# Layer 0's MLP: up tiles in pairs by seven half-width products, with weight sums, token sums and another order of the work

## The chip, the cores and the metric

The kernel runs on one core of one Trainium2 chip. The metric is the device time of one execution in microseconds. Engines are named as in the profile: PE is TensorE, DVE VectorE, ACT ScalarE, POOL GpSimd, SP SyncE, whose queue issues the loads.

## The reference, cut to what matters

Two layers act on 512 latent tokens; the first also on 256 context tokens with the same weights. Each layer is a set of token mixers and then an MLP with a gated residual. D_MODEL is 1024, D_FF 4096, all in float32.

```python
def sq_relu_mlp(h, w1, b1, w2, b2):
    a = jax.nn.relu(h @ w1 + b1)
    return (a * a) @ w2 + b2
...
        h2 = rmsnorm(x, ln2_g[l]) * (1.0 + sc2) + sh2
        x = x + g2 * sq_relu_mlp(h2, mlp_w1[l], mlp_b1[l], mlp_w2[l], mlp_b2[l])
        if with_ctx_out:
            ...
            xc = xc + cg2 * sq_relu_mlp(hc2, mlp_w1[l], mlp_b1[l], mlp_w2[l], mlp_b2[l])
```

sc2, sh2 and g2 come from a modulation product `silu(c) @ w_mod`, done per layer.

## The kernel before, in words

Activations lie with features on the partitions and tokens along the row: 768 tokens in layer 0 (pieces of 512 and 256 columns, `segs`), 512 in layer 1. Each float32 operand is split in two parts of the type that PE takes at full pace: a high part `H` and the rest, `L`. A product is three matmuls per block of 128 features: H·bH, H·bL, L·bH. `low` (L187) makes the split: a cast to H on ACT (L193) and a subtraction to L (`tt`, L177) on DVE, or on POOL for weights.

`load` (L307) takes one of four raw buffers (pool `raw`), issues a DMA of 512 x 128 weights on SP (L315) and splits it into one of six pairs `wH`, `wL`. A raw buffer is free again when its split on POOL is done. `proj` (L323) runs the matmuls of one output tile: per weight load and per piece 12 matmuls of 512 or 256 columns (`mm`, L215).

`mlp` (L1740) runs over eight chunks c. `up(c)` makes four tiles f of 128 hidden features: two loads and 48 matmuls (`proj`); ReLU with bias out of PSUM on ACT (`mr`), the square on POOL (`mq`), and its `low` with H on ACT and L on DVE (`aL`). Then `down(c-1)` uses the four tiles of the chunk before: for each of eight output tiles m one load of 512 x 128 of w2, 24 matmuls, and `residual` (L180, two pieces) on DVE, which adds the gated result into `xs[m]`. The last chunk's down product (`down_last`) runs within the first strand of the next layer. PSUM tiles come from small rings: the two pieces of a tile take a buffer of `p2`, of which there are two, so the products of tile m wait until the residual of tile m-2 has read its buffer.

The order on each engine is the order in which generators (strands) yield: `pipe` (L1484) turns among up to nine strands, here the output projection, the norms and the MLP; `run` (L1570) puts in one filling unit (`fill_step`) after every so many steps. The units of `mods` are the products for the next layer's modulation: `mod_units` (L1923) makes for each block j loads of 512 x 128 of w_mod, products of 32 rows (`mod__m`, L217), and an ending step. `prefetch` issues loads of coming units ahead, into the same raw buffers.

Of the kernel before, what the change touches and what calls it, by code (L numbers as in the profile page):

```python
# [22 lines left out]
P = 128  # L23
# [82 lines left out]
def hybrid_block(ctx: ExitStack, tc: tile.TileContext, I, C, out, dbg=None, stop=None):  # L106
# [12 lines left out]
    def uid(s):  # L119
        cnt[0] += 1  # L120
        return f"{ph[0]}__{s}_{cnt[0]}"

    def slot(dt=F32, name="s"):
        return sp.tile([P, TOT], dt, tag="t", name=uid(name), bufs=NT)

    def big(dt=F32, name="s"):
        return sp.tile([P, 1024], dt, tag="s", name=uid(name), bufs=NS)
# [13 lines left out]
    def yslot():  # L141
        return sp.tile([P, TOT], F32R, tag="y", name=uid("y"), bufs=8)
# [7 lines left out]
    def acc_tile(segs, filler=False):  # L150

        if filler:
            return [(t0, n, pf1()[:, :n]) for t0, n in segs]
        w, t = span(segs), p2()
        return [(w.start, w.stop - w.start, t[:, w])]
# [20 lines left out]
    def tt(o, a, b, op, eng=None):  # L176
        (eng or nc.vector).tensor_tensor(o, a, b, op)  # L177
# [10 lines left out]
    def low(H, L, src, heng=None, leng=None):  # L188

        if heng is nc.vector:  # L190
            nc.vector.tensor_copy(H, src)
        else:
            nc.scalar.copy(H, src)  # L193
        tt(L, src, H.bitcast(F32), ALU.subtract, eng=leng)
# [13 lines left out]
    def mm(ps, a, b, start, stop_, pos=None):  # L208
        n = int(np.prod(ps.shape[1:]))
        if a.dtype == F32R:  # L210
            cost = n * (0.43e-3 if n >= 256 else 1.7e-3)
        else:
            cost = max(n * 1.7e-3, 0.214)
        if pos is None:
            in_order(nc.tensor.matmul(ps, lhsT=a, rhs=b, start=start, stop=stop_), cost)  # L215
        else:
            in_order(nc.tensor.matmul(ps, lhsT=a, rhs=b, start=start, stop=stop_, tile_position=pos),  # L217
                     cost * ps.shape[0] / P)
# [82 lines left out]
    def rawtile():  # L301
        return rp.tile([P, 512], F32, tag="raw", name=uid("raw"))
# [6 lines left out]
    def load(src):  # L309

        raw = rawtile().rearrange("p (k n) -> p k n", k=4)
        if callable(src):
            src(raw)
        else:
            newest[0] = nc.sync.dma_start(raw, src.rearrange("(k p) n -> p k n", p=P))  # L315
        H, L = whalf()
        low(H, L, raw, leng=nc.gpsimd)
        return H, L
# [1 line left out]
    def wcols(src, x):  # L320
        return src[512 * x : 512 * x + 512]

    def proj(pieces, halves, mov):  # L323

        last_ = len(halves) - 1
        for x, half in enumerate(halves):
            if half is None:
                continue
            H, L = half
            for t0, n, ap in pieces:  # L330
                for a, c in [(t0, n)] if n <= 512 else [(t0, 512), (t0 + 512, n - 512)]:
                    ps, q = ap[:, a - t0 : a - t0 + c], slice(a, a + c)
                    for k in range(4):
                        bH, bL = mov(4 * x + k)
                        mm(ps, H[:, k, :], bH[:, q], x == 0 and k == 0, False)
                        mm(ps, H[:, k, :], bL[:, q], False, False)
                    for k in range(4):
                        mm(ps, L[:, k, :], mov(4 * x + k)[0][:, q], False, x == last_ and k == 3)
                    yield 0.0

    def now(g):
# [134 lines left out]
    def norm_piece(xs, a, piece, made, done, sc, sh, hH, hL):  # L476

        while piece not in made:
            yield 0.3
        pbf = yield from rms_stat(xs, a, *piece)  # L480
        yield from norm_mod(xs, [piece], pbf, sc, sh, hH, hL)
        done.add(piece)
# [225 lines left out]
    def hview(hH, hL):  # L708
        return lambda k: (hH[:, k, :], hL[:, k, :])
# [1027 lines left out]
                residual(xs[k], part, modT[l][:, 16:24, :], k)  # L1737
            made.add((t0, n))

    def mlp(l, vt, xs, mov, segs, near_end, first2, pieces, made, tail):  # L1740

        w = span(segs)
        g2 = modT[l][:, 40:48, :]

        gb = const(f"g2b{l}", [P, 16])
        gbv = gb.rearrange("p (k v) -> p k v", v=2)
        tt(gbv, g2, vt[:, vbase["mlp_b2"] : vbase["mlp_b2"] + KD].unsqueeze(2).to_broadcast([P, KD, 2]), ALU.mult)
        def weights1(f):
            return [load(wcols(I["mlp_w1"][l][:, f * P : (f + 1) * P], h)) for h in range(2)]

        def up(c):
            a, early = [], []
            for j in range(4):
                f = c * 4 + j
                if c == 0 and j < 3:
                    if j == 0:
                        W3 = [weights1(i) for i in range(3)]
                        early = [acc_tile(segs) for i in range(2)]

                        def third():  # L1760

                            while cur[0] is not None or cur[2] is not None:
                                yield 0.2
                            held[0] = True
                            early.append(acc_tile(segs, True))
                            return early[2], W3[2]

                        yield from first2(early[:2], W3[:2], mov, third)
                    elif j == 2:
                        held[0] = False  # L1770
                    ps = early[j]
                else:
                    ps = acc_tile(segs)
                    W = weights1(f)
                    yield from proj(ps, W, mov)
                r, q = slot(name="mr"), slot(name="mq")
                evac(r, ps, lambda d, a: act(d, a, AF.Relu, bias=vcol(vt, "mlp_b1", f)))
                tt(q[:, w], r[:, w], r[:, w], ALU.mult, eng=nc.gpsimd)
                H, L = yslot(), big(F32R, "aL")
                low(H[:, w], L[:, w], q[:, w])  # L1780
                a.append((H, L))
            return a

        def weights2(c, m):
            return load(I["mlp_w2"][l][c * 512 : (c + 1) * 512, m * P : (m + 1) * P])

        def down(c, a):
            for m in range(KD):
                ps = acc_tile(segs)
                W = weights2(c, m)  # L1790
                yield from proj(ps, [W], lambda k: a[k])
                if c == 0:
                    for t0, n in segs:
                        v = 0 if t0 == 0 else 1
                        q = slice(t0, t0 + n)
                        ts(xs[m][:, q], xs[m][:, q], gbv[:, m, v : v + 1], None, ALU.add)
                residual(xs[m], ps, g2, m)

        def down_last(a):
            last2 = []  # L1800
            for m in range(KD):
                if m in (1, 6):
                    near_end(m == 6)
                W, ps = weights2(7, m), acc_tile(segs)
                if m < KD - 2:
                    yield from proj(ps, [W], lambda k: a[k])
                    residual(xs[m], ps, g2, m)
                else:
                    last2.append((m, W, ps))
            for t0, n in pieces:  # L1810
                for m, W, ps in last2:
                    part = [(t0, n, cutout(ps, t0, n))]
                    yield from proj(part, [W], lambda k: a[k])
                    residual(xs[m], part, g2, m)
                made.add((t0, n))

        prev = None
        for c in range(8):
            a = yield from up(c)
            if prev is not None:  # L1820
                yield from down(c - 1, prev)
            prev = a
        tail.append(down_last(prev))


# [94 lines left out]
        for k in range(KD):  # L1920
            after(nc.sync.dma_start(xd[k][:, w], xs[k][:, w]), newest[0])

    def mod_units(l, js):  # L1923
        blocks = [mod_block(l, vts[l], j) for j in js]
        us = list(blocks[0][0])
        for a, b in zip(blocks, blocks[1:] + [None]):
            if b is not None:
                us += b[0]
            us.append(a[1])
        return us  # L1930

    def norms(pieces, made, sc, sh, hH, hL):
        hdone.clear()
        a = slot(name="ssq")
        return [norm_piece(xs, a, p, made, hdone, sc, sh, hH, hL) for p in pieces]

    def then(done, pieces, f):
        while not all(p in done for p in pieces):
# [5 lines left out]
    for l in range(DEPTH):  # L1944
# [71 lines left out]
        ts(modT[l][:, 16:24, :], modT[l][:, 16:24, :], 0.5, None, ALU.mult)  # L2016
        ph[0] = f"out{l}"
        if l + 1 < DEPTH:
            mods.extend(mod_units(l + 1, range(4)))
        hH = hp.tile([P, KD, TOT], F32R, tag="hH", name=uid("hH"))  # L2020
        hL = hp.tile([P, KD, TOT], F32R, tag="hL", name=uid("hL"))
        pieces = segs if len(segs) > 1 else [(0, 256), (256, 256)]
# [8 lines left out]
                prefetch()  # L2031
            ph[0] = mine

        body = mlp(l, vt, xs, hview(hH, hL), segs, next_layer, by_pieces(pieces, hdone), pieces, made, tail)
        run(f"mlp{l}", pipe(before + [body], 9), pace=PACE["mlp"])
        drain()


# [62 lines left out]
```

## Time and profile before

| | |
|---|---|
| median of 3 runs | 3291.99 us (3285.04 to 3303.0) |
| the profiled execution, time | 3282.8 us |
| its span, mean granted clock | 3281.0 us, 0.976 |
| layer 0's MLP, chunks 0 to 6 and the start of 7 | about 1351 to 1868 us |
| PE, DVE, ACT, POOL busy over the span | 94%, 41%, 35%, 42% |

The profile's page gives each engine's busy time; windows of the trace give the same for a stretch, with PE's granted clock (1.00 is full speed). A timeline row gives start, length, engine, line, operation, tile names and in brackets the idle time before it and what ended that. Matmuls overlap, so the pace of PE is read from the starts of successive matmuls, not from their lengths.

### The profile page before, as it was taken

The numbers are of one execution on the slowest core, as the hardware profiler recorded it, in microseconds if no ns is written. First come the engines' busy times: TensorE is split into PE (matmuls) and PEld (weight loads), VectorE is DVE, ScalarE is ACT, GpSimd is POOL, SyncE is SP. The second block draws the span as 40 slices with busy tenths as digits, with TensorE's granted clock in tenths as the row PEclk, the third lists the DMA queues.
The fourth block names the chain that finished last, engine by engine and source line by source line (L and its number), as shares of the span: only waits on it lengthen the run. The fifth ranks groups of instructions, "written<-read, shape, count | busy, mean of one in ns | idle before, by whom it ended". The sixth has DMA issues, their size and how long they took to land. (4 is left out here: it accounts for less than half of the span.)

```text
span 3281.0 us, 48633 instructions
## 1 busy us (share of the span) xinstructions
PE 3087.7 (94%) x18344; PEld 2614.1 (80%) x18344; DVE 1337.5 (41%) x2892; ACT 1135.7 (35%) x2137; POOL 1384.8 (42%) x1206
## 2 busy tenths in 40 slices
PE   7888989899999999999999997989998999999999
PEld 5777778788888888888888876777777788788887
DVE  6544422454444454511221265434354434442223
ACT  5435423234332122422222254333333432243333
POOL 4523332324344453443333355233333455555553
PEclk8999999999999999999999988999999999999999
DMA  8343443333243456222222334544343343823332
GB/s 269 102 115 114 124 147 94 106 101 95 78 147 92 137 173 198 68 78 75 71 74 75 95 99 121 145 136 113 100 113 98 104 137 116 273 84 97 97 97 81
DMA packets 556922, 380.24 MB, mean 116 GB/s; under 512 B 45177, under 2 KB 503870, under 8 KB 556688
## 3 DMA queue, kind: packets, MB, share of 16 engines
q1 hardware_dynamic: 556056, 376.98, 38.5%
q8 instruction: 145, 2.38, 0.3%
q14 instruction: 89, 0.73, 0.1%
q10 hardware_dynamic: 632, 0.16, 0.0%
HBM read 307.52 MB, written 63.75 MB: 113 GB/s over the span
## 5 line engine op out<-in xcount | busy, mean ns | idle before, releaser
L177 POOL TENSOR_TENSOR mlp__wL<-mlp__raw,mlp__wH 128x512 fp32r<-128x512 f32 x268 | 353.6, 1321 | 457.8 <-ACT mlp__wH L193 324.3
L193 ACT CAST mlp__wH<-mlp__raw 128x512 fp32r<-128x512 f32 x268 | 166.2, 621 | 505.3 <-PE mlp__p L215 340.6
L177 POOL TENSOR_TENSOR gt__wL<-gt__raw,gt__wH 128x512 fp32r<-128x512 f32 x128 | 167.4, 1313 | 240.1 <-ACT gt__wH L193 208.7
L215 PE MATMUL mlp__p<-out__hH,mlp__wH 128*128 128x512 f32 (+1 forms) x760 | 259.5, 353 | 0.5 <-ACT out__hH L518 0.5
L215 PE MATMUL mlp__p<-out__hL,mlp__wH 128*128 128x512 f32 (+1 forms) x760 | 256.5, 352 | 2.0 <-POOL out__hL L516 1.8
L180 DVE SCALAR_TENSOR_TENSOR mlp__x<-mlp__p,modT,mlp__x 128x512 f32<-128x512 f32 (+1 forms) x169 | 106.3, 657 | 338.3 <-PE mlp__p L215 332.1
L215 PE MATMUL mlp__p<-mlp__y,mlp__wH 128*128 128x512 f32 (+1 forms) x672 | 231.9, 356 | 0.0
L215 PE MATMUL mlp__p<-mlp__aL,mlp__wH 128*128 128x512 f32 (+1 forms) x672 | 231.2, 355 | 0.0
L177 DVE TENSOR_TENSOR mlp__aL<-mlp__mq,mlp__y 128x768 fp32r<-128x768 f32 (+1 forms) x64 | 82.4, 1287 | 304.3 <-ACT mlp__y L193 304.1
L215 PE MATMUL gt__m<-mod__hH,gt__wH 128*128 128x512 f32 (+1 forms) x512 | 172.1, 352 | 7.6 <-ACT mod__g L423 3.4
L215 PE MATMUL mlp__p<-out__hH,mlp__wL 128*128 128x512 f32 (+1 forms) x760 | 177.2, 350 | 0.0
L215 PE MATMUL gt__m<-mod__hL,gt__wH 128*128 128x512 f32 (+1 forms) x512 | 166.6, 341 | 0.0
L177 POOL TENSOR_TENSOR ml__wL<-ml__raw,ml__wH 128x512 fp32r<-128x512 f32 x64 | 83.9, 1311 | 189.8 <-ACT ml__wH L193 173.1
L215 PEld LDWEIGHTS mlp__p<-out__hH,mlp__wH 128*128 128x128 f32 x760 | 144.0, 189 | 22.0 <-issue 2.2
L215 PEld LDWEIGHTS mlp__p<-out__hL,mlp__wH 128*128 128x128 f32 x760 | 143.4, 190 | 22.4 <-POOL out__hL L516 2.2
L215 PE MATMUL mlp__p<-mlp__y,mlp__wL 128*128 128x512 f32 (+1 forms) x672 | 155.8, 354 | 0.0
L215 PEld LDWEIGHTS mlp__p<-out__hH,mlp__wL 128*128 128x128 f32 x760 | 130.0, 190 | 18.8
L215 PEld LDWEIGHTS mlp__p<-mlp__y,mlp__wH 128*128 128x128 f32 x672 | 126.8, 189 | 19.9 <-issue 2.2
L215 PEld LDWEIGHTS mlp__p<-mlp__aL,mlp__wH 128*128 128x128 f32 x672 | 127.1, 189 | 18.0
L193 ACT CAST gt__wH<-gt__raw 128x512 fp32r<-128x512 f32 x128 | 79.0, 619 | 173.1 <-DMA gt__raw<-in_w_in_dram 108.0
L215 PEld LDWEIGHTS mlp__p<-mlp__y,mlp__wL 128*128 128x128 f32 x672 | 115.0, 189 | 17.6
L215 PEld LDWEIGHTS gt__m<-mod__hH,gt__wH 128*128 128x128 f32 x512 | 98.3, 192 | 20.9 <-ACT mod__g L423 4.9
(574 smaller groups left out, 7915.5 us busy)
## 6 DMA issues: line engine op xcount, KB each, us to landing
mlp__raw<-in_mlp_w_dram SPq DMA_DIRECT2D x240, 256.0 KB
mod__raw<-in_w_mod_dram SPq DMA_DIRECT2D x160, 256.0 KB
gt__raw<-in_w_in_dram SPq DMA_DIRECT2D x128, 256.0 KB
ml__raw<-in_w_in_dram SPq DMA_DIRECT2D x64, 256.0 KB
hy__raw<-in_w_in_dram SPq DMA_DIRECT2D x48, 256.0 KB
spec<-spec__kk SPq DMA_DIRECT2D x80, 128.0 KB
ga__raw<-in_w_in_dram SPq DMA_DIRECT2D x32, 256.0 KB
hy__spec<-spec SPq DMA_DIRECT2D x16, 512.0 KB
```

The costliest lines, as they stand in the source:

```text
L177: (eng or nc.vector).tensor_tensor(o, a, b, op)
L180: nc.vector.scalar_tensor_tensor(o, a, s, b, op0, op1)
L193: nc.scalar.copy(H, src)
L215: in_order(nc.tensor.matmul(ps, lhsT=a, rhs=b, start=start, stop=stop_), cost)
```

## The change

It concerns layer 0 alone (`fast`). A chunk is now two up tiles, so there are 16 chunks. The first three (f below 6) are made as before, with the square in place of `mr`. Each of the 13 others is one `pair(f)`: the two tiles, the two halves of the 1024 input features and the two halves of the 768 tokens make a 2 x 2 by 2 x 2 block product, done by Strassen's scheme in Winograd's form with seven products of 384 columns. Each product is 12 matmuls. The four weight sums of a pair are additions on POOL, beside seven splits there; seven sums on DVE combine the products (`wx`, `wu`, `mr`) with ReLUs on ACT. The token sums (T1 to T4) are made once, by a strand `combos` in four rounds k, three operations of 768 and six of 384 columns on DVE in each, with casts on ACT. The squares of a pair are on ACT, in `finish_pair(0)`, called among the down products, which issues two squares and two casts; the two low parts follow at m of 2 and 4 (as called). `weights2` loads 256 x 256 for two m at once. `mod_units` no longer puts the ending of a block behind the start of the next.

```diff
+        def combos():
...
+            for k in range(4):
+                r, s, t = slot(name="tr"), slot(name="ts"), slot(name="tt")
+                tt(r[:, w], *whole(k), ALU.add)
+                tt(s[:, w], *whole(4 + k), ALU.add)
+                tt(t[:, lo_], r[:, hi_], r[:, lo_], ALU.subtract)
+                yield 3.0
...
+                low(H[:, w], L[:, w], t[:, w])
...
+                yield 6.0
+            T["all"] = True
+        def product(ps, W, mov_):
+            H, L = W
+            for k in range(4):
+                bH, bL = mov_(k)
+                mm(ps, H[:, k, :], bH, k == 0, False)
+                mm(ps, H[:, k, :], bL, False, False)
+            for k in range(4):
+                mm(ps, L[:, k, :], mov_(k)[0], False, k == 3)
+            yield 0.0
+        def pair(f):
+            while "all" not in T:
+                yield 0.3
+            if f == 6:
+                into_b12()
...
+            for i, x in ((0, 0), (1, 0), (1, 1), (0, 1)):
+                A[i, x] = slot(name="w1r")[:, :512] if i else rawtile()
...
+            W11 = split(A[0, 0])
+            tt(s1, A[1, 0], A[1, 1], ALU.add, eng=nc.gpsimd)
+            tt(A[1, 0], A[0, 0], A[1, 0], ALU.subtract, eng=nc.gpsimd)
+            tt(A[0, 0], s1, A[0, 0], ALU.subtract, eng=nc.gpsimd)
+            W2 = split(A[0, 0])
...
+            yield from product(pa, W11, b(0, 0))
+            nc.scalar.copy(x_[:, lo_], pa)
+            W1 = split(s1)
+            yield from product(pb_, W2, lambda k: T[2, k])
+            tt(x_[:, hi_], pb_, x_[:, lo_], ALU.add)
...
+        def finish_pair(m):
+            if m == 0:
+                for r, H, L in todo:
+                    act(r[:, w], r[:, w], AF.Square)
+                    nc.scalar.copy(H[:, w], r[:, w])
+            elif m in (2, 4) and todo:
+                r, H, L = todo.pop(0)
+                tt(L[:, w], r[:, w], H[:, w].bitcast(F32), ALU.subtract)
...
         def down(c, a):
             for m in range(KD):
+                finish_pair(m)
                 ps = acc_tile(segs)
                 W = weights2(c, m)
-                yield from proj(ps, [W], lambda k: a[k])
+                yield from proj(ps, [W], lambda k: a[k], step)
...
-            mods.extend(mod_units(l + 1, range(4)))
+            mods.extend(mod_units(l + 1, range(4), False))
...
-        run(f"mlp{l}", pipe(before + [body], 9), pace=PACE["mlp"])
+        run(f"mlp{l}", pipe(itertools.chain(before, [body], later(beside)), 9), pace=PACE["mlp"])
```

On DVE, the token sums (`tr`, `ts`, `tt`, `tc`) before the first pair, from the residual of output tile 7 (`out__x_12501`) of chunk 1's down product on; in the program before, none of these stand anywhere:

```order
L180 SCALAR_TENSOR_TENSOR mlp__x_12484<-mlp__p_2507_13525,modT_106,mlp__x_12484 128x256
L180 SCALAR_TENSOR_TENSOR out__x_12501<-mlp__p_2512_13548,modT_106,out__x_12501 128x512
L180 SCALAR_TENSOR_TENSOR out__x_12501<-mlp__p_2512_13548,modT_106,out__x_12501 128x256
L400 TENSOR_REDUCE mod__s_2543_13650<-mod__m_13645 128x8
L177 TENSOR_TENSOR modT_107<-mod__s_2543_13650,vec_490 128x8
L177 TENSOR_TENSOR mlp__tc_13574<-mlp__ts_13654,mlp__tc_13573 128x384
L177 TENSOR_TENSOR mlp__tr_13695<-out__hH_12074,out__hL_12075 128x768
L177 TENSOR_TENSOR mlp__ts_13696<-out__hH_12074,out__hL_12075 128x768
L177 TENSOR_TENSOR mlp__tt_13697<-mlp__tr_13695 128x384
L177 TENSOR_TENSOR mlp__t_2526_13576<-mlp__ts_13696,mlp__tr_13695 128x384
```

The fourth round (`tr_13695` on) stands behind the last residual; the three before it stand among the residuals of the same down product, behind the low part of tile 4.

On SP (line numbers are the changed kernel's), the loads between the last weights of chunk 1's down product (`mlp__raw_13526`, L1924) and those of the first pair (L1817); `mod__raw` are modulation weights, of which 13 stand there in a row:

```order
L1924 DMA mlp__raw_13526<-in_mlp_w_dram 128x2x256
L411 DMA mod__raw_13544<-in_w_mod_dram 128x4x128
...
L411 DMA mod__raw_13720<-in_w_mod_dram 128x4x128
L1817 DMA mlp__raw_13730<-in_mlp_w_dram 128x4x128
L1817 DMA mlp__w1r_13732<-in_mlp_w_dram 128x4x128
L1817 DMA mlp__w1r_13734<-in_mlp_w_dram 128x4x128
L1817 DMA mlp__raw_13736<-in_mlp_w_dram 128x4x128
```

The pair's loads have moved behind thirteen of the filling units' loads, which take the same ring of raw buffers.

On DVE, a later chunk, from the last sums of a pair to the residuals of the down product beside it (`x_12077` is output tile 0, `x_12142` tile 1, `x_12211` tile 2). Before:

```order
L180 SCALAR_TENSOR_TENSOR mlp__x_12077<-mlp__p_2576_13956,modT_106,mlp__x_12077 128x512
L180 SCALAR_TENSOR_TENSOR mlp__x_12077<-mlp__p_2576_13956,modT_106,mlp__x_12077 128x256
L177 TENSOR_TENSOR mlp__aL_13953<-mlp__mq_13949,mlp__y_13952 128x768
L180 SCALAR_TENSOR_TENSOR mlp__x_12142<-mlp__p_2580_13989,modT_106,mlp__x_12142 128x512
L180 SCALAR_TENSOR_TENSOR mlp__x_12142<-mlp__p_2580_13989,modT_106,mlp__x_12142 128x256
```

and now:

```order
L177 TENSOR_TENSOR mlp__mr_16224<-mlp__p_2992_16219,mlp__wu_16222 128x384
L177 TENSOR_TENSOR mlp__mr_16223<-mlp__p_2991_16218,mlp__wu_16222 128x384
L180 SCALAR_TENSOR_TENSOR mlp__x_12077<-mlp__p_3008_16340,modT_106,mlp__x_12077 128x512
L180 SCALAR_TENSOR_TENSOR mlp__x_12077<-mlp__p_3008_16340,modT_106,mlp__x_12077 128x256
L177 TENSOR_TENSOR mlp__aL_16333<-mlp__mr_16223,mlp__y_16332 128x768
L177 TENSOR_TENSOR mlp__aL_16335<-mlp__mr_16224,mlp__y_16334 128x768
L180 SCALAR_TENSOR_TENSOR mlp__x_12142<-mlp__p_3012_16361,modT_106,mlp__x_12142 128x512
L180 SCALAR_TENSOR_TENSOR mlp__x_12142<-mlp__p_3012_16361,modT_106,mlp__x_12142 128x256
```

Both low parts of a pair stand between the residuals of tiles 0 and 1; this is so in ten of the 13 chunks, and in three one of them stands behind tile 1's residual.

## Rows read from the trace of the kernel before

**Rows 1.** Page, engines: busy us (share) x instructions; windows: us, PE, PEld, DVE, ACT, POOL, PEclk, DMA, GB/s
```profile
PE 3087.7 (94%) x18344; PEld 2614.1 (80%) x18344; DVE 1337.5 (41%) x2892; ACT 1135.7 (35%) x2137; POOL 1384.8 (42%) x1206
...
1450.00:1550.00 100.00, 100.00 (x602) 86.55 (x601) 17.50 (x26) 25.34 (x40) 39.02 (x29) 1.00 0.25 73
1850.00:1950.00 100.00, 88.91 (x493) 72.60 (x492) 53.44 (x110) 39.55 (x73) 40.71 (x36) 0.90 0.41 119
```

**Rows 2.** Timeline of PE, one tile of a down product: start, us, engine, line, operation
```profile
1519.31 0.40 PE L215 MATMUL mlp__p<-mlp__y,mlp__wH 128*128 128x512 f32 x1
...
1522.06 0.28 PE L215 MATMUL mlp__p<-mlp__y,mlp__wH 128*128 128x256 f32 x1
...
1523.49 0.40 PE L215 MATMUL mlp__p<-out__hH,mlp__wH 128*128 128x512 f32 x1
```

**Rows 3.** Lines by form, PE: group | busy us, mean ns of one | idle before
```profile
L215 PE MATMUL mlp__p<-mlp__y,mlp__wL 128*128 128x512 f32 x224 | 59.9, 389 | 0.0
...
L215 PE MATMUL mlp__p<-mlp__y,mlp__wL 128*128 128x256 f32 x224 | 36.0, 283 | 0.0
...
L215 PE MATMUL wa__p<-wa__wkL,wa__wqX 128*128 128x384 f32 x32 | 10.8, 336 | 0.0
```

**Rows 4.** Timeline of DVE, the residual of that tile
```profile
1523.70 1.14 DVE L180 SCALAR_TENSOR_TENSOR out__x<-mlp__p,modT,out__x 128x512 f32<-128x512 f32 x2 [3.04 <-PE mlp__p L215]
```

**Rows 5.** Timelines of DVE and POOL at two places, subtractions beside each other
```profile
1256.15 1.43 POOL L177 TENSOR_TENSOR mlp__wL<-mlp__raw,mlp__wH 128x512 fp32r<-128x512 f32 x1 [2.28 <-ACT mlp__wH L193]
1256.35 2.05 DVE L177 TENSOR_TENSOR mg0x__mL<-mg0x__ac,mg0x__y 128x768 fp32r<-128x768 f32 x1
...
1377.76 4.03 DVE L177 TENSOR_TENSOR mlp__aL<-mlp__mq,mlp__y 128x768 fp32r<-128x768 f32 x2 [7.22 <-ACT mlp__y L193]
1378.96 2.02 POOL L177 TENSOR_TENSOR mlp__wL<-mlp__raw,mlp__wH 128x512 fp32r<-128x512 f32 x1
...
1380.93 2.18 POOL L177 TENSOR_TENSOR mlp__mq<-mlp__mr 128x768 f32<-128x768 f32 x1
```

**Rows 6.** Groups: layer 0's low parts (least/median/most ns); then lines by form as above
```profile
L177 DVE TENSOR_TENSOR mlp__aL<-mlp__mq,mlp__y x32: 946/959/2054, 1377.8 to 1838.6; 128x768 fp32r<-128x768 f32 x32
...
L177 DVE TENSOR_TENSOR ml__mW<-ml__mW,ml__kq 128x384 f32<-128x384 f32 x16 | 8.8, 547 | 0.3 <-ACT ml__mW L184 0.3
...
L193 ACT CAST mlp__y<-mlp__mq 128x768 fp32r<-128x768 f32 x32 | 26.7, 834 | 50.1 <-POOL mlp__mq L177 50.1
...
L184 ACT ACTIVATE mlp__mr<-mlp__p,vec 128x768 f32<-128x768 f32 x31 | 27.8, 898 | 18.7 <-PE mlp__p L215 18.7
```

**Rows 7.** Timelines of POOL, SP, ACT and PE: one turn of a raw buffer; modulation products
```profile
1490.19 1.29 POOL L177 TENSOR_TENSOR mlp__wL<-mlp__raw,mlp__wH 128x512 fp32r<-128x512 f32 x1 [1.31 <-ACT mlp__wH L193]
1491.50 0.37 SPq L315 DMA_DIRECT2D mlp__raw<-in_mlp_w_dram  x1
...
1494.46 0.62 ACT L193 CAST mlp__wH<-mlp__raw 128x512 fp32r<-128x512 f32 x1 [0.69 <-DMA mlp__raw<-in_mlp_w_dram]
...
1867.81 1.08 PE L217 MATMUL mod__m<-mod__raw,scp 128*32 128x128 f32 x32
```

**Rows 8.** Timeline of PE and windows (columns as in Rows 1) at the seam to layer 1
```profile
1873.72 0.80 PE L215 MATMUL wa__p<-mlp__y,wa__wH 128*128 128x512 f32 x1 [3.78 <-ACT wa__wH L193]
1876.00:1879.00 3.00, 3.00 (x8) 2.31 (x7) 0.00 (x0) 1.00 (x2) 1.58 (x2) 0.50 0.91 254
...
1894.66 1.07 PE L215 MATMUL spec__m<-spec__h,spec__mw 64*64 64x512 f32 x2 [1.48 <-ACT spec__h L558]
1897.00:1900.00 3.00, 3.00 (x10) 2.52 (x10) 2.23 (x5) 1.25 (x2) 1.96 (x2) 0.50 0.00 0
...
1938.00:1939.00 1.00, 0.00 (x0) 0.00 (x0) 1.00 (x3) 0.00 (x0) 1.00 (x2) 1.00 1.00 328
```

## What the change does to the time, predicted before it ran

> **What bounds the kernel now.** I read the table of engines first: TensorE is busy 94% of the span, VectorE 41%, GpSimd 42% [rows 1]. Then the stretches: in the middle of layer 0's MLP, 1450 to 1550 us, TensorE is busy 100.00 of 100 us at a granted clock of 1.00, with GpSimd at 39 us and VectorE at 17.5 [rows 1]. There nothing but products sets the time, so a product removed there comes straight off, provided no new wait opens. At the seam to layer 1, 1850 to 1950 us, it is busy 88.9 us at 0.90 [rows 1]: there time goes to waits and to the clock.
>
> Next the pace. One tile of a down product before is 12 matmuls of 512 columns and 12 of 256: they start at 1519.31, at 1522.06 and the next group at 1523.49 [rows 2]. So 512 columns cost 2.75/12 = 229 ns, 256 columns 1.43/12 = 119 ns, a tile 4.18 us. The mean lengths of one matmul are longer, 389 and 283 ns, since they overlap; one of 384 columns is 336 ns, midway between the two [rows 3]. I put its pace midway too: 174 ns. The residual of a tile starts 0.2 us after its products end and takes 1.14 us for its two pieces [rows 4].
>
> **The change, part by part.**
>
> *Products.* A pair of up tiles takes 96 matmuls before, four times 4.18 = 16.72 us. Now it takes 7 products of 12 matmuls of 384 columns: 84 x 174 ns = 14.62 us. That saves 2.1 us in each of 13 pairs: **-27.2 us**. The bounds of the 384-column pace are small (each 5 ns is 5.5 us over all 1092 matmuls); I keep -22 to -32.
>
> *Token sums before the first pair.* A round of them is three subtractions or additions 768 wide, at 0.95 us like the low part of an activation, and six 384 wide at 547 ns [rows 6]: 6.1 us on VectorE. The first three rounds stand between the residuals of the down tiles of chunk 1, the fourth behind the last residual. From the low part of tile 4 to that residual VectorE has 8 residuals (9.1), three rounds (18.4) and a low part (0.95): 28.5 us. TensorE has left at that point some 4 us of tile 5 and 8 x 2.09 = 16.7 us of down tiles. A down tile may not start before the residual two tiles earlier has freed its PSUM buffer, so the last tile ends about 8 us late. Behind it the SP queue holds 13 loads of modulation weights ahead of the pair's four, and the raw ring has four buffers, so three load turns pass before W11 has landed. A turn, from the end of one GpSimd split to the ScalarE cast of the load that it freed, is 1491.48 to 1494.46, 2.98 us [rows 7]: 8.9 us, plus cast 0.62 and split 1.29. The second product waits for three GpSimd sums and one more cast and split, 5.8 us. So 16.6 us in all, in which TensorE does 1.5 us of modulation products (32 take 1.08 us [rows 7]) and one product of 2.1: 13 us idle. With the 8 before, 21 us idle. Ends: 12 if the loads and rounds move up, 32 if each turn also waits behind the fourth round on ScalarE. Behind an idle of 3.78 us at the seam the clock fell: the matmul at 1873.72 took 0.80 us, and 0.50 was granted to 1879 [rows 8], 5.3 us at half speed, 2.7 lost. I add 3: **+24 us**, 12 to 35.
>
> *Waits in each chunk.* This is the term I am least sure of. The down product of a chunk now has 12 matmuls a tile, 2.09 us, not 4.18. VectorE, which had one low part to fit between residuals, gets the two of a pair back to back, in 10 of 13 chunks between the residuals of tiles 0 and 1, in three apart. Tile 3 needs the buffer that tile 1's residual frees. It could start 6.27 us after tile 0 began. Tile 0's residual ends 2.09 + 0.2 + 1.14 = 3.43 us after that moment, then come the two low parts, A long together, then tile 1's residual, 1.14, and 0.1 to the start: 4.67 + A. So the stall is s = A - 1.6 us. One low part alone takes 0.95 us [rows 6]; one that met a GpSimd split took 2.05; two back to back with GpSimd at work all along took 4.03, while a GpSimd split and square beside them took 2.02 and 2.18 instead of 1.3 [rows 5]. GpSimd gets seven splits and four sums a pair, 1.3 us each, and four splits for the down weights, some 20 of the 31.4 us, and its squares leave it. Nor can the second low part start before ScalarE has done two squares and two casts, 0.90 + 0.83 each [rows 6], behind the last sum and relu of the pair (about 1.1): 4.6 us after tile 0 began, so A is at least 2.1. So A is 2.1, 3.25 or 4.03, s is 0.5, 1.65 or 2.4. I take 1.6, the middle, for the ten and 0.4 for the three: **+17.2 us**. Ends 5 (all in GpSimd's pauses) and 30 (all against it). Before, a tile of 4.18 us left slack for all of this, and [rows 1] shows it as 100.00 us busy. The Trainium skill, "SBUF — State Buffer", section "Who interferes with whom", says that VectorE and GpSimd share a port as an exclusive lock and the loser fully blocks. By that a split met at its start would cost its whole 1.3 us, s about 1.8 and the term 19; the 4.03 us for two agrees in size.
>
> *Clock.* A 1.48 us gap at 1894.66 was followed by 0.50 granted from 1897 to 1900; a gap of the whole of 1938 to 1939 was followed by none, 1.00 [rows 8]. The new stalls of 1.65 us lie between. 3 us at half speed is 1.5 us lost; a third of ten chunks, **+5 us**, 0 to 15.
>
> *Activations.* Beyond that bound on A the squares on ScalarE cost nothing: relus, squares and casts are about 5 us a chunk on an engine that had 25 busy of 100 [rows 1]; if that cover is gone, the casts of weights come late. The seven combining sums, 547 ns each, stand within products of 2.09 us: nothing.
>
> *Seam to layer 1.* The 3.78 us wait and its 2.7 us of half clock may go, because the modulation loads are done earlier. Against this the last chunk now brings 16.7 us of down products, not 33.4, to cover the norm and the filters of layer 1. I set **0**, -6 to +6.
>
> *Sum.* -27.2 + 24 + 17.2 + 5 + 0 = +19 us. The profiled execution took 3282.8; the sum gives 3301.8. The median of the runs shown is 9.2 higher, 3291.99, and the sum by it **3311**.
>
> **The rivals.**
>
> *A, faster or no slower.* GpSimd's pauses. The low parts fall where GpSimd waits for ScalarE's cast (in the profile its splits show 1.31 and 2.28 us of idle before them [rows 5, 7]), A is 2.1 and s 0.5 in the ten chunks: +5. Rounds and loads of the first pair overlap, 12 idle. The clock stays. Then -27.2 + 12 + 5 = -10, with the seam's gain of 6 -16, and where the first pair's idle is covered altogether -22 or less: 3265 to 3282. It decides at an A of about 2.5 us, s 0.9, where with 12 idle the sum is -6: below it the products' gain shows. For it: GpSimd is busy only two thirds of a chunk. Against it: the casts of the next pair's weights come just then, so splits are likely there.
>
> *B, much slower.* The clock falls after nearly every stall of a chunk, and A is 4.03: -27.2 + 24 + 26 + 15 = +38, 3330. For it: the gap of 1.48 us [rows 8]. Against it: the 1 us gap. The Trainium skill, "TensorE: Matmul & The Clock Gate", section "A second HAM failure mode: psum-queue depth-cycling", describes a kernel in which small idle times between groups, from cycling PSUM buffers, made the clock swing between its levels. By that rule, too, the time would be that of B; here the 1938 gap speaks against it and the 1894 gap for it.
>
> *C, no difference.* One of the two stalls is small: s about 0.7 for the steady chunks, or the first pair idle 12 rather than 21: +5, 3297.
>
> *D, the change gives less than its count.* 384 columns go at the pace of their length against that of 512, 229 x 336/389 = 198 ns, not 174: 2.0 us less saved a pair, +26 on the forecast, 3337. For it: the lengths [rows 3] are all that there is on 384 columns. Against it: by length alone 256 columns would take 167 ns, and they take 119 [rows 2].
>
> **How the numbers follow.** What a measurement can tell from no change is about 0.5%, 16.5 us. The forecast (+10 to +28) has 0.38, A 0.27, B 0.1, C 0.2, D 0.05. Of the forecast two thirds lie above +16.5, 0.25; with B, D and the upper edge of C 0.41 is slower. Faster by over 16.5 needs the first pair's idle covered, or A with the seam's gain: 0.2, most of A. The rest, 0.39, is no difference. The range runs from A's better end, 3265, to B's middle with a little more, 3338; it leaves out A with neither stall, and B with D.
>
> **What would show it.** Right: TensorE no longer at 100.00 in a 100 us stretch of layer 0's MLP, with idle of about 1.6 us before the fourth down tile, released by VectorE's residual; low parts of 1.5 to 2 us each; one gap of about 20 us in pieces before the first 384-column product; products of 384 columns every 174 ns. Wrong: the per-chunk idle below 0.5 us (then A holds), low parts at 0.95; a granted clock of 0.50 in many slices of the MLP (then B); no gap before the first pair, or products at 198 ns. If another wait shows, on ScalarE's casts of weights or on a load, my cover for activations and loads was wrong.

## The result, and where the time went in the profile after

The changed kernel takes 3314.87 us (median of 5 runs, 3311.58 to 3319.05); the kernel before took 3291.99 (3285.04 to 3303.0) beside it. The ratio is 1.0069, 95% interval 1.0052 to 1.0085: some 23 us slower. The forecast was 3311. One of e5's eleven executions below took 5021 us at a granted clock of 0.555 and is left out of its time and ratio.

Both traces can be cut at the same four places: the first product of the output projection, the first of the MLP, the last that the MLP itself issues (the last chunk's down product lies behind it), and the first product of layer 1's global attention. The times are differences of the starts in PE's timelines; of the MLP's last product the end is taken. Column e4 is the kernel before, profiled once more; the rest belongs to the experiments below.

| us | before | e4 | after | e1 | e2 | e3 | e5 | e6 | e7 | e8 | e9 |
|---|---|---|---|---|---|---|---|---|---|---|---|
| up to the output projection | 1328.8 | 1339.2 | 1339.2 | 1326.8 | 1331.5 | 1337.3 | 1332.3 | 1334.4 | 1336.4 | 1334.4 | 1327.1 |
| MLP of layer 0 | 516.7 | 517.5 | 549.5 | 533.8 | 558.3 | 550.6 | 523.5 | 541.1 | 528.0 | 535.5 | 529.4 |
| to layer 1's attention | 339.6 | 336.1 | 323.5 | 315.0 | 318.0 | 324.5 | 323.4 | 320.7 | 320.1 | 323.0 | 319.0 |
| sum of these two | 856.3 | 853.6 | 873.0 | 848.8 | 876.3 | 875.1 | 846.9 | 861.8 | 848.1 | 858.5 | 848.4 |
| PE idle in the MLP (waits over 0.2 us) | 0.4 | 0.4 | 30.1 | 18.4 | 30.1 | 9.2 | 9.0 | 2.2 | 12.2 | 16.8 | 11.8 |

The first line says how much single executions differ: it is the same code in all columns, and takes 1327 to 1339 us. So the two profiled executions, 3282.8 and 3316.6, are not simply subtracted: 10 of their 34 us come ahead of any changed instruction. The sum of the MLP and what follows it is free of that: 873.0 against 855.0 (mean of the two of before), +18. In all kernels but that of before (columns before and e4), 16.7 us of down products have moved from the third line to the second, since the last chunk is half as long.

Page, engines, changed kernel [rows 1]:

```profile
PE 3086.0 (93%) x18188; PEld 2628.2 (79%) x18188; DVE 1486.0 (45%) x3147; ACT 1198.0 (36%) x2240; POOL 1469.9 (44%) x1271
```

PE's busy time hardly moved. From the MLP's start to the first gate product of layer 1 it did fall by 27.9 us, from 615.1 to 587.2 by windows of the two traces; elsewhere it rose by 26, of which 7.6 ahead of the output projection, where no instruction differs.

Windows of the same kernel (us, PE, PEld, DVE, ACT, POOL, PEclk, DMA share, GB/s), the first pair and a later stretch; they answer to the 100.00 busy us of [rows 1]:

```profile
1440.00:1460.00 20.00, 14.88 (x111) 11.66 (x109) 18.57 (x34) 4.55 (x9) 0.00 (x0) 1.00 0.04 13
1460.00:1480.00 20.00, 9.50 (x89) 6.02 (x81) 7.84 (x13) 5.22 (x14) 5.23 (x5) 0.74 0.65 184
...
1700.00:1750.00 50.00, 48.70 (x278) 44.19 (x277) 26.20 (x43) 18.69 (x28) 30.59 (x23) 1.00 0.16 48
```

Timelines of PE and SP at the first pair (start, us, engine, line, operation, idle before it and what ended that):

```profile
1444.33 0.50 PE L215 MATMUL mlp__p<-mlp__y,mlp__wH 128*128 128x512 f32 x1 [2.72 <-DVE mlp__x L180]
...
1462.63 0.42 PE L217 MATMUL mod__m<-mod__raw,scp 128*32 128x128 f32 x8 [2.47 <-DMA mod__raw<-in_w_mod_dram]
...
1473.60 0.69 PE L215 MATMUL mlp__p<-out__hH,mlp__wH 128*128 128x384 f32 x1 [2.58 <-ACT mlp__wH L193]
...
1479.90 1.08 PE L215 MATMUL mlp__p<-mlp__y,mlp__wH 128*128 128x384 f32 x4 [2.31 <-ACT mlp__wH L193]
...
1446.41 22.21 SPq L411 DMA_DIRECT2D mod__raw<-in_w_mod_dram  x11
1470.10 0.37 SPq L1817 DMA_DIRECT2D mlp__raw<-in_mlp_w_dram  x1
```

This is the first-pair wait as it was forecast: five waits for residuals behind the token sums (6.5 us), then eleven modulation loads that hold SP's queue for 22 us before the pair's first load goes out, waits for those loads, and the first two products late for their weights: 17.0 us idle from 1438 to 1480. PE's busy time in the five four-microsecond windows from 1464 to 1484, taken times what its clock lacked, gives 4.5 us more.

Waits of PE, 1485 to 1900 us (engine line <- releaser: us in total, times, longest):

```profile
PE mlp__p L215 <- DVE mlp__x L180: 12.2, 11, 2.5
```

Timelines of ACT, DVE, PE and POOL at three of these stalls (of the first, only ScalarE's cast ahead of it):

```profile
1529.94 0.62 ACT L193 CAST mlp__wH<-mlp__raw 128x512 fp32r<-128x512 f32 x1 [2.71 <-PE mlp__p L215]
...
1564.65 0.62 ACT L193 CAST mlp__wH<-mlp__raw 128x512 fp32r<-128x512 f32 x1 [2.73 <-DMA mlp__raw<-in_mlp_w_dram]
1565.18 0.84 ACT L184 ACTIVATE mlp__mr<-mlp__mr 128x768 f32<-128x768 f32 x1
...
1568.33 1.83 DVE L177 TENSOR_TENSOR mlp__aL<-mlp__mr,mlp__y 128x768 fp32r<-128x768 f32 x2 [2.06 <-ACT mlp__y L1875]
1571.26 0.50 PE L215 MATMUL mlp__p<-mlp__y,mlp__wH 128*128 128x512 f32 x1 [1.98 <-DVE mlp__x L180]
...
1832.41 1.92 POOL L177 TENSOR_TENSOR mlp__raw<-mlp__ws,mlp__raw 128x512 f32<-128x512 f32 x1
...
1832.22 2.92 DVE L177 TENSOR_TENSOR mlp__aL<-mlp__mr,mlp__y 128x768 fp32r<-128x768 f32 x2
...
1836.25 0.50 PE L215 MATMUL mlp__p<-mlp__y,mlp__wH 128*128 128x512 f32 x1 [0.93 <-DVE mlp__x L180]
1836.58 0.39 PE L215 MATMUL mlp__p<-mlp__aL,mlp__wH 128*128 128x512 f32 x1
```

There are eleven such stalls, 12.2 us in all, each before the fourth down tile; the first and the last of the 13 pairs have none. They have two kinds. The last eight (0.27 to 0.93 us, 5.8 in all) are as forecast: two low parts that met GpSimd take 2.36 to 2.93 us, not 1.83. The first three (1.94, 1.98, 2.47) are not: there the low parts run at or near their full pace (1.83 for two; 1.13 for the one that stands ahead of tile 1's residual in the third), and VectorE waits for ScalarE. ScalarE holds square and cast behind the cast of a weight that has to wait: in the second and third for its load (2.73 and 3.44 us), in the first for PE (2.71 us). From 1590 to 1891 us no modulation load goes out, and from 1602 us to the MLP's end no weight's cast waits over 1 us for its load, so the late loads end where the large stalls end. That the modulation loads make the weights late is read from this, not tested.

A stall costs more than the idle shown. Down tiles start 2.10 us apart; before the last stall the next start was due at 1867.70, and it came at 1868.78, 1.08 us later, where the profile shows 0.93 idle, since the matmul before overlaps. The matmul after it follows 0.34 us later instead of 0.23 (0.33 in the rows above, from 1836.25 to 1836.58). That is 0.26 us beyond the idle, 2.9 us if all eleven cost as much.

The pace of the new products, timeline of PE:

```profile
1547.12 0.34 PE L215 MATMUL mlp__p<-out__hH,mlp__wH 128*128 128x384 f32 x1
...
1548.34 0.33 PE L215 MATMUL mlp__p<-out__hL,mlp__wH 128*128 128x384 f32 x1
```

Seven steps in 1.22 us: 174 ns.

### The profile page after: what moved, and what is told of

Its sections match the earlier page's. It is cut to its first block, busy times and chain, and to the rows that moved or that the text cites. A ratio compares the mean times of both kernels' runs of the same rounds, so it can differ in the third digit from the quotient of the medians.

```text
span 3314.8 us, 48774 instructions
## 1 busy us (share of the span) xinstructions
PE 3086.0 (93%) x18188; PEld 2628.2 (79%) x18188; DVE 1486.0 (45%) x3147; ACT 1198.0 (36%) x2240; POOL 1469.9 (44%) x1271
## 3 DMA queue, kind: packets, MB, share of 16 engines
q8 instruction: 144, 2.36, 0.3%
## 5 line engine op out<-in xcount | busy, mean ns | idle before, releaser
L215 PE MATMUL mlp__p<-mlp__y,mlp__wH 128*128 128x512 f32 (+2 forms) x808 | 270.1, 356 | 21.1 <-DVE mlp__x L180 18.7
L180 DVE SCALAR_TENSOR_TENSOR mlp__x<-mlp__p,modT,mlp__x 128x512 f32<-128x512 f32 (+1 forms) x281 | 169.1, 637 | 240.6 <-PE mlp__p L215 234.2
L215 PE MATMUL mlp__p<-mlp__aL,mlp__wH 128*128 128x512 f32 x704 | 245.2, 356 | 0.0
L215 PE MATMUL mlp__p<-out__hH,mlp__wH 128*128 128x512 f32 (+2 forms) x552 | 196.3, 359 | 3.1 <-ACT mlp__wH L193 2.6
L215 PE MATMUL mlp__p<-mlp__y,mlp__wL 128*128 128x512 f32 x756 | 196.6, 353 | 0.0
L215 PE MATMUL mlp__p<-out__hL,mlp__wH 128*128 128x512 f32 (+2 forms) x552 | 193.6, 359 | 2.6 <-POOL out__hL L516 1.8
L177 DVE TENSOR_TENSOR mlp__aL<-mlp__mr,mlp__y 128x768 fp32r<-128x768 f32 (+1 forms) x64 | 86.6, 1366 | 153.1 <-ACT mlp__y L193 144.5
L215 PE MATMUL mlp__p<-out__hH,mlp__wL 128*128 128x512 f32 (+2 forms) x552 | 133.3, 356 | 0.0
L215 PEld LDWEIGHTS mlp__p<-out__hL,mlp__wH 128*128 128x128 f32 x552 | 104.5, 191 | 14.5 <-POOL out__hL L516 2.2
L215 PE MATMUL gt__m<-mod__hH,gt__wL 128*128 128x512 f32 (+1 forms) x512 | 110.8, 339 | 0.0
```

The lines of the kernel that those rows point to most:

```text
L180: nc.vector.scalar_tensor_tensor(o, a, s, b, op0, op1)
```

## The experiments

**e1, low parts later.** On VectorE alone, the two low parts of a pair are pinned behind residuals:

```diff
...
-            elif m in (2, 4) and todo:
+            elif m in (4, 6) and todo:
                 r, H, L = todo.pop(0)
-                tt(L[:, w], r[:, w], H[:, w].bitcast(F32), ALU.subtract)
+                after(nc.vector.tensor_tensor(L[:, w], r[:, w], H[:, w].bitcast(F32), ALU.subtract), lastres[0])
```

> The changed kernel with one thing moved: the two low parts of a pair are pinned on VectorE behind the residuals of down tiles 3 and 5, where the code asks for them, not between those of tiles 0 and 1. My theory (the per-chunk stall is A - 1.6 us, A the time from residual 0 to the end of the second low part): the 12 stalls of 0.3 to 2.5 us before a down tile, 13.1 us in the changed kernel's trace, fall under 0.3 us each; time 3315 - 13 = 3302, between 3299 and 3305. Rival (the chunk is bound by something beside them, weight casts behind loads, so the wait only changes its name): PE idle in the 12 chunks stays above 9 us and the time within 5 us of 3315.

Measured: 3289.52 us (11 runs), 0.9991 of before (0.998 to 1.0003). Waits of PE from 1470 us to the end of the MLP:

```profile
PE mlp__p L215 <- ACT mlp__wx L1842: 0.5, 1, 0.5
```

The stalls are gone, so the rival falls. (The twelve stalls and 13.1 us of the expectation are eleven and 12.2 in the trace.) The gain is larger than expected. The MLP took 15.7 us less: 11.7 us of idle, 1.4 of low clock (in windows of half a microsecond), and 2.6 more, about what the eleven stalls cost beyond their idle. Another 8.5 us are in the stage behind it; e5 and e7, which issue the same work there, took 320 to 323, so that part is the spread of executions and not shown to be the edit's.

**e2, sums early.**

```diff
-        run(f"mlp{l}", pipe(itertools.chain(before, [body], later(beside)), 9), pace=PACE["mlp"])
+        run(f"mlp{l}", pipe(itertools.chain(before, later(beside), [body]), 9), pace=PACE["mlp"])
```

> The changed kernel with the strand of token sums placed ahead of the MLP's strand, so that the four rounds lie in chunks 0 and 1 and no filling units are taken while waiting for them. My theory (token sums late, then 13 modulation loads ahead of the pair's): the 17.0 us of PE idle between 1436 and 1480 us and the 4.5 us lost there at the lower clock vanish, up to 6.5 us come back at the seam where the modulation products are now left over; 3315 - 21 = 3294, at most 3300. Rival (the sums cost VectorE the same wherever they lie, because residuals queue behind them): idle of over 6 us appears in chunks 0 and 1, and the gain stays under 10 us, 3305 or more.

Measured: 3303.8 us, 1.0032 (1.002 to 1.0045), 11 us less than the changed kernel and between the two expectations. The trace does not show these 11 us as a gain of the edit: the MLP took 8.8 us more, MLP and next stage together 876.3 against 873.0, and what was shorter are stages that the edit doesn't touch (the first by 7.7). The first pair's idle went, but the modulation loads, no longer taken in one pile, lay among the chunks up to 1752 us, and the waits from 1470 us on grew to 21.6 us. Its worst stall, in timelines of SP, ACT, DVE and PE, and then the window behind it:

```profile
1752.03 0.37 SPq L411 DMA_DIRECT2D mod__raw<-in_w_mod_dram  x1
...
1762.16 0.62 ACT L193 CAST mlp__wH<-mlp__raw 128x512 fp32r<-128x512 f32 x1 [2.20 <-DMA mlp__raw<-in_mlp_w_dram]
...
1764.45 3.06 DVE L177 TENSOR_TENSOR mlp__aL<-mlp__mr,mlp__y 128x768 fp32r<-128x768 f32 x2 [4.12 <-ACT mlp__y L1875]
...
1768.61 0.80 PE L215 MATMUL mlp__p<-mlp__y,mlp__wH 128*128 128x512 f32 x1 [4.72 <-DVE mlp__x L180]
```

```profile
1769.00:1773.00 4.00, 4.00 (x13) 3.37 (x13) 0.75 (x3) 0.57 (x1) 2.21 (x2) 0.50 0.09 29
```

A weight comes late, its cast holds ScalarE's queue, the squares and casts behind it come late, then the low parts, then the residual, then PE, and then the clock halves. The rival's sign came true as well: before 1470 us PE is idle for 8.6 us, of which 2.5 for a norm on VectorE beside the first round of sums and 3.6 for a residual behind the second. And some 17 us were lost in the MLP to the low clock, against 7 in the changed kernel (windows of half a microsecond).

**e3, halved chunks without pairs.**

```diff
-            if fast and c >= 3:
+            if False:
...
-        if fast:
+        if False:
             strands.append(combos())
...
```

> The changed kernel without pairs and token sums: 16 chunks of two tiles, each made as before (48 matmuls, square on GpSimd), w2 loaded 256 x 256. My theory (all of the change's price hangs on the pairs: late sums, low parts back to back): as fast as before, 3292 within 6 us. Rival (halving the chunk has a price of its own, the seam's cover and a residual every 2.09 us): 3300 or more, with the extra time at the seam or as stalls of VectorE's residuals in each chunk.

Measured: 3315.16 us, 1.006 (1.0048 to 1.0073). My theory falls: with no pair at all, the chunks of two tiles cost as much as the whole change. 8.2 us are five waits for residuals, the longest 2.81; the rest of the 17 us that the MLP takes beyond 516.7 + 16.7 is the low clock behind one of them and small losses (e6). e3 keeps the change's 256 x 256 loads of w2, its square in place and its order of the modulation units, so this is the price of all four together; which part of it is the halving's alone was not tested.

**e4, the kernel before again,** without an edit.

> The kernel before, unchanged, for a second trace: how much the stages differ between two executions of the same program. The stage up to the output projection took 1328.8 us in the trace of before and 1339.1 in that of the changed kernel, with the same instructions. My theory (that is noise of an execution): it lies anywhere between 1325 and 1342 here, and the time from the start of layer 0's MLP to the last chunk's down product at 516.6 within 2 us. Rival (the changed kernel slows code that it does not touch): the first stage within 2 us of 1328.8 again.

Measured: 3293.78 us, a single run. The first stage took 1339.2 us here and the MLP 517.5: the theory holds, and the table's first line shows the range.

**e5, the edits of e1 and e2 together.**

> Both moves together: token sums ahead of the MLP's strand (as in e2) and low parts pinned behind the residuals of tiles 3 and 5 (as in e1). In e2 the first pair's idle went, but the stalls of a chunk grew from 13.1 to some 20 us, since the modulation loads then lay between the chunks, and the granted clock fell behind those over 3 us. My theory (two causes of the loss, that mask each other in e2): with the low parts out of the way both go, PE idle in the MLP under 8 us in all, time 3290 - 17 = 3273, between 3266 and 3280, faster than before. Rival (modulation loads among the chunks delay the weights themselves, so something else waits): over 15 us of idle remain, 3285 or more.

Measured: 3283.6 us (ten runs), 0.9976 (0.9965 to 0.9988). Window from behind the first pair to the end of the MLP:

```profile
1500.00:1878.00 378.00, 378.00 (x2259) 345.44 (x2258) 185.49 (x303) 145.40 (x230) 228.91 (x172) 1.00 0.28 83
```

PE is never idle for 378 us. The modulation loads are still among the chunks, so weights and squares still come late at times, but nobody waits: the low parts are due a whole pair later. Idle in the MLP is 9.0 us, all ahead of this window and a little over the 8 expected; the time is 4 us above the range that I gave.

**e6, e3 with late low parts.** As e3, with e1's pin for the classic tiles from the second chunk on:

```diff
...
-            low(H[:, w], L[:, w], r[:, w])
+            if late:
+                nc.scalar.copy(H[:, w], r[:, w])
+                todo.append((r, H, L))
+            else:
+                low(H[:, w], L[:, w], r[:, w])
...
-                squared(r, a)
+                squared(r, a, fast and c > 0)
```

> As e3 (16 chunks of two tiles, no pairs), with the low parts of the two tiles pinned behind the residuals of tiles 3 and 5 from the second chunk on. e3 took 3315 with 9.2 us of stalls behind residuals. My theory (of the price of halved chunks, two thirds are these stalls with the clock behind them): 3300, between 3296 and 3305, with no stall of a residual over 0.5 us. Rival (the price is more and shorter accumulations on PE and the shorter cover at the seam): 3309 or more. Against e1 it also says what seven products for eight are worth alone: e6 less e1, plus the 21 us of the first pair, should be 27.

Measured: 3301.47 us, 1.0027 (1.0015 to 1.0038); no stall of a residual, 2.2 us idle. The medians of e3 and e6 are 14 us apart; 9.5 of these are in the MLP, and those are the stalls and the low clock behind one of them. The rest lies in stages that differ from execution to execution. The MLP still takes 541.1 instead of 516.7 + 16.7 = 533.4. Of these 7.7 us, 1.8 are idle, 1.9 are 36 more matmuls of modulation products that now lie in the MLP (at 44 and 88 ns), and down tiles of this length mostly start 2.10 to 2.12 us apart where half of a tile of [rows 2] is 2.09, 1 to 4 us over 120 tiles. Without stalls, pairs (e5) against none (e6) are 523.5 against 541.1, that is 17.6; with e5's 6.8 us more of idle added, and 4.6 for its clock (0.86 between 1372 and 1384, 0.83 between 1400 and 1420), it is 29, close to the 27.2 of the products. (The sum that I had set, e6 less e1 by their medians and 21, gives 33.)

**e7, loads of the first pair first.** As e1, with the wait moved:

```diff
         def pair(f):
-            while "all" not in T:
-                yield 0.3
-            if f == 6:
-                into_b12()
...
             yield from product(pa, W11, b(0, 0))
             nc.scalar.copy(x_[:, lo_], pa)
+            while "all" not in T:
+                yield 0.3
+            if f == 6:
+                into_b12()
```

> As e1, but the first pair's loads, the split of W11 and its first product stand ahead of the wait for the token sums, so that the modulation loads come behind the pair's. My theory (of the first pair's 17 us idle, 6.5 come from residuals queued behind the sums and the other 10.5 from the load turns): the wait of the first 384-column product for its weights goes; PE idles for the second product until the fourth round of sums is done, some 5 to 8 us later than the last residual, so 5 us are gained: 3285. Rival (the filling units that are taken while the strand waits, not the load turns, hold PE): no gain, 3290 within 2, with the same idle under another name.

Measured: 3287.19 us, 0.9983 (0.9971 to 0.9995), between the two expectations; by these ratios e7 and e1 do not differ clearly. In the traces the MLP took 5.8 us less than e1's. The first product's wait is gone; the second waits for the last sums' cast:

```profile
1473.58 0.69 PE L215 MATMUL mlp__p<-mlp__tc,mlp__wH 128*128 128x384 f32 x1 [3.94 <-ACT mlp__tc L193]
```

The edit also changed the order on VectorE: all four rounds of sums now stand behind the last residual, where in e1 three stand among the residuals.

```profile
1448.14 1.14 DVE L1715 SCALAR_TENSOR_TENSOR out__x<-mlp__p,modT,out__x 128x512 f32<-128x512 f32 x2 [0.96 <-PE mlp__p L215]
1449.20 1.55 DVE L177 TENSOR_TENSOR mlp__tr<-out__hH,out__hL 128x768 f32<-128x768 f32 x1
```

With that the waits for residuals fell from 6.4 us in e1 to 0.3, and this makes up the 6.2 us less idle (12.2 against 18.4). The waits for the pair's weights (5.1 us in e1) went, but 4.3 us for the last sums stand in their place, and modulation products wait for their loads as before (6.8 us, 6.1 in e1). So the part that I had put to the load turns did not fall: there the rival is right, the idle stands under another name. Load turns and late sums hold the first pair at the same time, and freeing the one shows the other.

**e8, squares on GpSimd.** As e1, with

```diff
-                    act(r[:, w], r[:, w], AF.Square)
+                    tt(r[:, w], r[:, w], r[:, w], ALU.mult, eng=nc.gpsimd)
```

> As e1, with the squares of a pair back on GpSimd (in place), still issued in finish_pair. My theory (with the low parts out of the way nobody waits for a pair's activations within its chunk, so their engine costs nothing): 3290 within 4. Rival (GpSimd is the next bound: 7 splits, 4 sums, 4 splits and 2 squares are 23 to 25 of 30 us in order, so weights come late): over 1 us of PE idle per chunk behind weight casts, 3302 or more.

Measured: 3295.73 us, 1.0014 (0.9997 to 1.003), 1.7 us outside my range. The trace has 16.8 us idle in the MLP against e1's 18.4 and no stall per chunk; the MLP is 1.7 us longer, with 3.5 us more of low clock. That excludes the rival's 3302; 6 us between the medians are not explained by any wait, so whether the squares' engine matters by a few us stays open.

**e9, sums only in up products.** As e5, with

```diff
             for k in range(4):
+                while T.get("go", 0) <= k:
+                    yield 0.3
...
-                yield 6.0
+                yield 2.0
             T["all"] = True
...
+            T["go"] = 2 * c
             a = yield from up(c)
```

> As e5 (sums early, low parts late), with the rounds of token sums let go only at the start of the up products of chunks 1 and 2, two rounds each, where fewer residuals queue. In e5 the MLP still had 9.0 us of idle, of which 2.5 (norm of the context tokens behind the first round), 3.6 and its half clock (residual behind the second) belong to the sums. My theory: 5 us of idle and 3 of clock less, 3284 - 7 = 3277, faster than before by 0.4%. Rival (the sums take VectorE 24 us wherever they are, and the down product of chunk 0, whose residuals come with the bias additions, has no room for any): idle in the MLP stays at 8 us or more, 3284 within 3.

Measured: 3277.65 us, 0.9959 (0.9945 to 0.9973), the fastest. The time is as forecast, the reason is not: idle in the MLP is 11.8 us, four waits of 2.7 to 3.1, as the rival said, and MLP and next stage together, 848.4, are no better than e5's 846.9. The first stage, which no edit touches, was 5 us shorter. So e5 and e9 both beat the kernel before, and which of the two is better isn't shown.

## Why the prediction was right, term by term

*Products, -27.2.* Right: 174 ns as taken, and a pair that has no modulation product in it takes 14.57 us in e5's trace, against 16.72.

*First pair, +24.* Right in place and size: 17.0 us idle and 4.5 of clock, 21.5 in all. I had put 8 us down to the residuals (6.5 were), 13 to load turns and weights (10.5). The wait for the second product was 2.3 us and not the 3.7 that my 5.8 less 2.1 makes, because the first ran at half clock and took 4.0 us. The mechanism holds in part: in e7, with the pair's loads first, the late sums hold its products for 4.3 us where the weights held them for 5.1 in e1, and I had put this part to the load turns and weights alone.

*Stall in each chunk, +17.2.* Too high, 12.2 idle, or 15.1 with the 2.9 that the stalls cost beyond it. The place and the releaser are right, and e1 shows it: with the low parts moved the stalls vanish. The step that set A failed in part. Contention gave A of 2.4 to 2.9 in eight chunks, between my 2.1 and 3.25; there the idle is A less 2.0 in seven of the eight, not A less 1.6. In the three longest, A was set through ScalarE's queue by a weight's cast that had to wait, of which I had only said that casts of weights come late if its cover is gone: I had priced the squares on ScalarE at nothing beyond a bound, and not what stands ahead of them in its queue. Nor did the 0.4 us hold for the three chunks whose low parts stand apart: two have no stall, and one has the longest. The Trainium skill, "SBUF — State Buffer", section "Who interferes with whom", says that a VectorE instruction with two inputs in SBUF contends with a GpSimd instruction that reads SBUF, and that the shared ports are an exclusive lock. The trace agrees: two low parts of 1.83 us alone took 2.92 (0.95 and 2.05), and the GpSimd sum beside them 1.92 instead of 1.3, in size as if each waited for the other to end. The Trainium skill has "fully blocks" there for VectorE's 2-port modes, not for such a subtraction.

*Clock, +5.* Smaller: of the eleven stalls only the 1.98 us one was followed by a low clock (0.96 over 1560 to 1600, 1.6 us). Rival B did not occur here, but e2 shows it: there the clock fell behind six of the seven stalls of over 1 us from 1500 us on (1.77 to 4.72; not behind 1.23), and behind those over 3 us PE starts at half clock at once.

*Seam, 0.* The stage behind the MLP took 323.5, against 336 to 340 less the 16.7 that moved: some 2 us more, within the spread.

*What I left out.* Chunks of half the length have a price without any pair. e3 and e6 show it: stalls, which I had counted, and 7.7 us more in e6's MLP, of which I had counted nothing. In the changed kernel this is 1.9 us of modulation products and about 2 without a place. These, the 2.9 that the stalls cost beyond their idle, the seam and the norm made up for the 11 us by which I had set the first pair, the idle of the stalls and the clock too high. So the total came out closer than its terms, by luck. The sum from the trace is -27.2 + 21.5 + 12.2 + 2.9 + 1.6 + 2.4 (seam) + 0.5 (waits for the norm at the start) + 1.9 = 15.8; the stages show +18, and the medians say 23 with a spread of 5.

## What to carry to other kernels

A reduction of PE's products is worth its count only where the side engines' work keeps its distance in time: halving the products per residual took away the slack that had hidden one subtraction, and an in-order queue turned a late load into a stall three engines further on. Before writing the products off, look for work in a queue that is not due yet (here the low parts, due only after the next pair) and pin it behind what is due: that alone brought the time back to that of the kernel before. Work done while a strand waits can take loads and buffers ahead of what the strand waits for (here eleven loads, 22 us of SP's queue); putting the loads first helps only if nothing else holds the same product (e7).

## What was not expected of the hardware

The clock fell after some stalls and not after others of about the same length: in the changed kernel after 1.98 us (0.96 granted over 1560 to 1600) but not after 2.47 us (1.00 over 1600 to 1650), in e3 after the wait of 2.67 us (0.96 over 1480 to 1520) but not after that of 2.81 us (1.00 over 1560 to 1640). Behind each of e2's four waits over 3 us the first matmul already took 0.79 or 0.80 us, but a wait of 3.10 us in e9 was followed by no low clock, and in e2 waits of 1.77, 1.84 and 2.18 us were. So the length of the wait alone does not tell it. And the same instructions ahead of the output projection took 1327 to 1339 us, a spread of 0.9%.
